# Attention values split inside their own head pair: a change to the emission order of a hybrid decoder block

## The chip, the cores and the metric

The kernel runs on one core of one Trainium2 chip. The metric is the device time of one execution in microseconds (us). Six queues matter in what follows. TensorE (PE) multiplies matrices; its weight loads are shown apart as PEld. VectorE (DVE), ScalarE (ACT) and GpSimd (POOL) do elementwise work. SyncE (SP) issues nearly all DMA transfers. Each engine takes its instructions strictly in the order in which the program emits them, so an instruction that waits holds up everything behind it on its engine.

## The reference

The block mixes tokens by dilated sliding-window attention and by a causal convolution, joins the two with sigmoid gates, and then runs a SwiGLU feed-forward network. Only the attention matters here. There are three groups of eight heads of width 64, with a window and a dilation for each group. Every group gives an output and a log denominator, and the three groups are merged per head with a softmax over these denominators:

```python
s = jnp.einsum('brnqhd,brnkhd->brnhqk', qb, kb) * (Dh ** -0.5) + bias
s = jnp.where(valid[:, None], s, NEG_INF)
lse = jax.nn.logsumexp(s, axis=-1)
p = jnp.exp(s - lse[..., None])
o = jnp.einsum('brnhqk,brnkhd->brnqhd', p, vb)
...
alpha = jax.nn.softmax(jnp.stack(lses, axis=0), axis=0)
o = jnp.einsum('gbsh,gbshd->bshd', alpha, jnp.stack(outs, axis=0))
```

Sequence length and model width are 1024; all inputs are float32.

## The kernel before

Every product is made of three matrix products of a rounded high part and a low part (`hi*hi + hi*lo + lo*hi`), so each operand has to be split by two instructions first: a copy that rounds (`hi`, on ACT) and a subtraction (`lo`, on DVE or POOL).

The stages follow each other: projections and the convolution, then the value projections (`v`, L843 to L877), two late gates, the convolution's output product (eight column tiles, `unit`, matmuls at L287, L289, L291), the attention's output product, the mixing product and the feed-forward part. Attention has no stage of its own. It is a Python generator, `attention` (L882), and `beat` advances it by one `yield` after about every third matmul of the value projections (`RATE` 0.33) and after about every 1.5 matmuls later (0.66). Its instructions are thus threaded between the filler matmuls on every engine, in the order of emission. There is no scheduler beyond that. A second clock, `tick`, comes once for each three matmuls and drives the background generators: weight splits, `conv_norm`, `conv_split` and the merges.

Attention works through 12 head pairs, called (group, pair) here: (0,0) to (2,3), eight query blocks `u` each, 96 steps `s` in all. One step emits the scores of block `s` (`att_s`: four matmuls at L937, bias and minimum on DVE at L940), the exponentials of block `s-1` (`att_e`, ACT L950), the transposes of block `s-3` (`att_t`: PE L973, split on ACT L978 and DVE L979) and the product with the values of block `s-4` (`att_p`: PE L994 and L996, reduction on DVE L1001). After `att_e` of the last block of a pair in groups 0 and 1 the statistics go to memory (`tokens_out`, L959 or L963), and after `att_p` of the last block the outputs do.

Three helpers feed a pair:

- `stacks` (from L790) loads queries and keys of the next pair: four query loads of 256 KB (L799, L800), two key loads of 512 KB (L801) and the bias (L458). POOL then copies the query halves across partitions in eight casts (L806, L807). It is emitted when the running pair has passed its block 1 (`u == 2`).
- `values` (L820) loads the values of the next pair (L826, L829 or L831) from the memory tensor to which `v` stored them (L850).
- `value_parts` (L834) splits one half of these values: a copy on ACT (L839) and a subtraction on POOL (L840).

In the kernel before, `values` for the next pair is emitted at block 4 of the running pair, and its two `value_parts` at blocks 6 and 7 of the running pair. For the very first pair the load is emitted only when `conv_norm` has ended, and the generator then lets 12 beats pass.

In group 2, when a pair is done, `others` (L811) loads statistics (L815) and outputs (L817) of the two other groups, and `merge` (L1010) is started as a background generator: minimum over the groups (L1018), weights (L1019 to L1025), three scaled outputs (L1029; group 0 on POOL, the others on DVE), two additions (L1031, L1033), and eight transposes with their split (L1040, L1043, L1044).

SP issues DMAs in emission order. The transfers share eight semaphore lanes in turn, so a transfer also waits for the one issued eight places before it.

Of the kernel before, what the change touches and what calls it, by code (L numbers as in the profile page):

```python
# [54 lines left out]
def f(ap):  # L55
    return ap.bitcast(F32)


class Build:
# [730 lines left out]
    def stacks(self, g, hp):  # L790
# [17 lines left out]
        st = self.tiny(96, "stat", 3).rearrange("p (g u e) -> p g u e", g=3, u=8)  # L808
        return [g, hp, ops, bt, st, []]

    def others(self, p):  # L811

        hp, st, outs = p[1], p[4], p[5]
        for i in range(2):
            self.nc.sync.dma_start(st[:, i], self.d_st[i, hp].rearrange("(p u) e -> p u e", u=8))  # L815
            outs.append(self.slot())
            self.nc.sync.dma_start(outs[i].rearrange("p (u e) -> p u e", u=8),  # L817
                                   self.d_att[i, hp].rearrange("(p u) e -> p u e", u=8))
# [63 lines left out]
    def attention(self, after):  # L882

        live, s, total = {}, 0, 96
        order = [(g, hp) for g in range(3) for hp in range(4)]
        nxt, cur, u, x, V = self.stacks(*order.pop(0)), None, 8, None, []
        while s < total + self.LP:
            if s < total:
                if x is None and nxt and u > 3 and nxt[0] * 2 + nxt[1] // 2 < self.vn:
                    x = self.values(*nxt[:2])  # L890
                elif u in (6, 7) and x is not None:
                    V.append(self.value_parts(x, u - 6))
                if u == 8:
                    while after in self.gens or nxt[0] * 2 + nxt[1] // 2 >= self.vn:
                        yield 0
                    if x is None:
                        x = self.values(*nxt[:2])
                        for _ in range(12):
                            yield 0
                    while len(V) < 2:  # L900
                        V.append(self.value_parts(x, len(V)))
                    now, cur, u, nxt, x, V = V, nxt, 0, None, None, []
                live[s] = a = {}
                self.att_s(a, cur, now, u)
                u += 1
                if u == 8:
                    cur[2] = cur[3] = now = None
                if u == 2 and order:
                    nxt = self.stacks(*order.pop(0))
            if s % 8 == 1 and s > 64 and live[s - 2]["p"][0] == 2:  # L910
                self.others(live[s - 2]["p"])
            if 0 <= s - 1 < total:
                self.att_e(live[s - 1])
            yield 0
            if 0 <= s - self.LT < total:
                self.att_t(live[s - self.LT])
                yield 0
            if 0 <= s - self.LP < total:
                yield from self.att_p(live.pop(s - self.LP))
            s += 1  # L920
# [89 lines left out]
    def merge(self, hp, st, O):  # L1010


        nc = self.nc
        t = self.tiny(96, "mrg", 2)
        m, r = (t[:, i * 16:(i + 1) * 16].rearrange("p (u e) -> p u e", u=8) for i in range(2))
        w = t[:, 48:].rearrange("p (g u e) -> p g u e", g=3, u=8)
        low, tot = st[:, :, :, 0:2], st[:, :, :, 2:4]
        nc.vector.tensor_reduce(m, low.rearrange("p g u e -> p u e g"), AX.X, OP.min)  # L1018
        nc.vector.tensor_tensor(w, low, m.unsqueeze(1).to_broadcast([128, 3, 8, 2]), op=OP.subtract)  # L1019
        nc.scalar.activation(t[:, 48:], t[:, 48:], AF.Exp, scale=-1.0)  # L1020
        yield 2
        nc.vector.tensor_tensor(tot, tot, w, op=OP.mult)
        nc.vector.tensor_reduce(m, tot.rearrange("p g u e -> p u e g"), AX.X, OP.add)
        nc.vector.reciprocal(r, m)
        nc.vector.tensor_tensor(w, w, r.unsqueeze(1).to_broadcast([128, 3, 8, 2]), op=OP.mult)  # L1025
        for g in range(3):
            y = O[g].rearrange("p (u h c) -> p u h c", u=8, h=2)
            a = w[:, g].unsqueeze(3).to_broadcast([128, 8, 2, 64])
            (nc.gpsimd if g == 0 else nc.vector).tensor_tensor(y, y, a, op=OP.mult)  # L1029
            yield 1  # L1030
        nc.vector.tensor_tensor(O[1], O[1], O[2], op=OP.add)  # L1031
        yield 1
        nc.vector.tensor_tensor(O[0], O[0], O[1], op=OP.add)  # L1033
        yield 3
        hi, lo = self.slot(F32R), self.slot(F32R)
        for h in range(2):
            ps = self.bank("t")
            for i in range(4):
                u = h * 4 + i
                nc.tensor.transpose(ps[:, i * 128:(i + 1) * 128], O[0][:, u * 128:(u + 1) * 128], self.ident)  # L1040
            y = ps.rearrange("p (u m) -> p u m", u=4)
            a, b = (x.rearrange("p (m u) -> p u m", u=8)[:, h * 4:h * 4 + 4] for x in (hi, lo))
            nc.scalar.copy(a, y)  # L1043
            nc.vector.tensor_tensor(b, y, f(a), op=OP.subtract)  # L1044
            yield 2
        self.OT[hp] = hi, lo

# [154 lines left out]
def build(ctx, tc, aps):  # L1202
    B = Build(ctx, tc, aps)
# [93 lines left out]
    B.finish(conv)  # L1297
    assert bl not in B.gens
    B.banks(g=2, s=2, t=2, o=2)
    B.OT, B.merges = {}, []  # L1300
    cn = B.bg(B.conv_norm())
    att = B.attention(cn)
# [11 lines left out]
    for n in range(LATE):  # L1314
        w = B.weights(late[n])
        s = B.slot()
# [10 lines left out]
    def gate_load(d):  # L1327
        c = B.slot()
        nc.sync.dma_start(c, d)
        return c  # L1330

    nxt = gate_load(B.d_gc[0])
    ws = {}

    for n, hf in [(0, 0), (1, 0), (0, 1), (1, 1)] + [(n, hf) for n in range(2, 8) for hf in range(2)]:
        if hf == 0:
            ws[n] = B.weights(co[n])
            mg[n] = nxt
            nxt = gate_load(B.d_gc[n + 1]) if n < 7 else (gate_load(B.d_ga[0]), gate_load(B.d_gc[0]))
# [4 lines left out]
        ps = B.unit(ws[n], B.rhs(B.cop[hf]), KT)  # L1344
# [21 lines left out]
    for n in range(8):  # L1366
# [4 lines left out]
        for hf in range(2):  # L1371
            s = slice(hf * H, (hf + 1) * H)
            ps = B.unit(w, lambda kt: tuple(x[:, s] for x in B.OT[kt]), 4)
            nc.vector.tensor_tensor(c[:, s], ps, c[:, s], op=OP.mult)
            nc.vector.tensor_tensor(c[:, s], c[:, s], y[:, s], op=OP.add)
            x = B.slot(F32R)
# [4 lines left out]
    y = None  # L1381
# [173 lines left out]
    for j in range(PLAIN, FT):  # L1555
        s = [None, None]
        p, odd = divmod(j, 2)
# [231 lines left out]
```

## Time and profile before

| what | value |
|---|---|
| time, median of 3 runs | 1787.02 us (1786.26 to 1789.1) |
| the profiled execution | 1787.76 us, span 1786.0 us |
| PE busy, share of the span | 1725.8 us, 97% |
| DVE, ACT, POOL busy | 70%, 44%, 28% |
| first and last value matmul (L863) starts | 563.9 us and 803.6 us |
| first score matmul (L937), last value product (L994) start | 635.1 us and 950.4 us |
| transposes of the merges (L1040) | 902.1 us to 968.0 us |

The span starts at the first instruction. A row of the timeline gives start, duration, engine, line of the kernel, operation, and in brackets how long the engine had sat idle before and what released it. A row of the windows gives the busy time of each engine in a stretch, the granted TensorE clock as a share of full speed (PEclk), the busy share of the DMA engines, and the rate. Matmuls overlap, so a row's duration is longer than the distance to the next one.

### The profile page before, as it was taken

The numbers are of one execution on the slowest core, as the hardware profiler recorded it, in microseconds if no ns is written. First come the engines' busy times: TensorE is split into PE (matmuls) and PEld (weight loads), VectorE is DVE, ScalarE is ACT, GpSimd is POOL, SyncE is SP. The second block draws the span as 40 slices with busy tenths as digits, with TensorE's granted clock in tenths as the row PEclk, the third lists the DMA queues.
The fourth block names the chain that finished last, engine by engine and source line by source line (L and its number), as shares of the span: only waits on it lengthen the run. The fifth ranks groups of instructions, "written<-read, shape, count | busy, mean of one in ns | idle before, by whom it ended". The sixth has DMA issues, their size and how long they took to land.

```text
span 1786.0 us, 24511 instructions
## 1 busy us (share of the span) xinstructions
PE 1725.8 (97%) x8698; PEld 1462.3 (82%) x8698; DVE 1251.7 (70%) x2198; ACT 790.9 (44%) x1549; POOL 505.8 (28%) x357
## 2 busy tenths in 40 slices
PE   8989999999999989999898999999999999999998
PEld 6768888887777989998687888888888888878886
DVE  6899867899996546555676475586566565567686
ACT  6344344334433456556553145653333333353453
POOL 0067777877773223332320040040000000000000
PEclk9999999999999989999889999999999999999999
DMA  4333334556667576667753753203223223395234
GB/s 159 140 118 123 119 118 147 154 165 174 186 165 224 161 215 181 190 186 232 264 182 104 261 193 107 100 36 123 89 89 140 90 89 124 130 333 170 95 134 148
DMA packets 185783, 274.94 MB, mean 154 GB/s; under 512 B 56113, under 2 KB 107948, under 8 KB 185660
## 3 DMA queue, kind: packets, MB, share of 16 engines
q1 hardware_dynamic: 185020, 272.74, 47.6%
q8 instruction: 68, 1.11, 0.3%
q10 hardware_dynamic: 576, 0.56, 0.1%
q14 instruction: 55, 0.45, 0.1%
q0 software_dynamic: 64, 0.07, 0.0%
HBM read 183.76 MB, written 94.28 MB: 156 GB/s over the span
## 4 chain that ended last, share of the span: by engine, by line
PE 64%; DVE 5%; DMA 3%; ACT 2%; issue 1%; POOL 0%; SPq 0%; DVEq 0%; ACTq 0%; POOLq 0%
PE p L1673 12%; PE p L305 8%; PE p L303 8%; PE p L304 8%; PE p L1409 5%; PE p L291 3%; PE p L289 3%; PE p L287 3%; PE p L865 3%; PE p L867 3%; PE p L863 2%; PE p L937 2%; PE p L973 1%; PE p L996 1%; DMA b<-dv 1%
## 5 line engine op out<-in xcount | busy, mean ns | idle before, releaser
L303 PE MATMUL p<-b,b 128*128 128x512 f32 x1204 | 471.1, 391 | 14.0 <-DVE c L777 7.3
L305 PE MATMUL p<-b,b 128*128 128x512 f32 x1204 | 470.1, 390 | 0.4 <-POOL b L180 0.4
L304 PE MATMUL p<-b,b 128*128 128x512 f32 x1204 | 470.0, 390 | 0.0
L303 PEld LDWEIGHTS p<-b,b 128*128 128x128 f32 x1204 | 226.9, 188 | 64.8 <-DVE c L777 9.2
L305 PEld LDWEIGHTS p<-b,b 128*128 128x128 f32 x1204 | 227.0, 189 | 48.9 <-POOL b L180 1.5
L304 PEld LDWEIGHTS p<-b,b 128*128 128x128 f32 x1204 | 226.9, 188 | 46.7
L179 ACT CAST b<-b 128x1024 fp32r<-128x1024 f32 x129 | 135.6, 1051 | 181.0 <-POOL b L200 71.0
L1673 PE MATMUL p<-b,b 128*128 128x512 f32 x924 | 209.7, 389 | 1.5 <-DVE c L1582 1.5
L180 POOL TENSOR_TENSOR b<-b,b 128x1024 fp32r<-128x1024 f32 x72 | 175.6, 2438 | 115.7 <-ACT b L179 99.7
L1673 PEld LDWEIGHTS p<-b,b 128*128 128x128 f32 x924 | 173.3, 188 | 37.9 <-DVE c L1582 1.9
L637 DVE SCALAR_TENSOR_TENSOR p<-b,par,p 128x511 f32<-128x511 f32 (+14 forms) x232 | 163.6, 738 | 0.0
L180 DVE TENSOR_TENSOR b<-b,b 128x1024 fp32r<-128x1024 f32 x57 | 69.7, 1223 | 123.8 <-ACT b L179 123.8
L287 PE MATMUL p<-b,b 128*128 128x512 f32 x368 | 152.7, 415 | 0.8 <-DVE b L1348 0.8
L291 PE MATMUL p<-b,b 128*128 128x512 f32 x368 | 150.9, 410 | 0.0
L289 PE MATMUL p<-b,b 128*128 128x512 f32 x368 | 150.5, 409 | 0.0
L1052 DVE TENSOR_TENSOR b<-c,b 128x512 fp32r<-128x512 f32 x125 | 90.7, 736 | 39.7 <-ACT b L1051 39.4
L863 PE MATMUL p<-b,b 128*128 128x256 f32 x384 | 114.7, 299 | 2.2 <-DVE c L783 2.2
L865 PE MATMUL p<-b,b 128*128 128x256 f32 x384 | 114.7, 299 | 0.9 <-DVE b L173 0.9
L867 PE MATMUL p<-b,b 128*128 128x256 f32 x384 | 114.0, 297 | 0.0
L1051 ACT CAST b<-c 128x512 fp32r<-128x512 f32 x125 | 76.5, 618 | 56.0 <-DVE c L355 17.6
L979 DVE TENSOR_TENSOR c<-p,c 128x256 fp32r<-128x256 f32 (+1 forms) x96 | 52.3, 545 | 68.5 <-ACT c L978 60.2
L1409 PE MATMUL p<-b,b 128*128 128x512 f32 x384 | 88.9, 391 | 0.0
(222 smaller groups left out, 3042.6 us busy)
## 6 DMA issues: line engine op xcount, KB each, us to landing
b<-w_in SPq DMA_DIRECT2D x53, 512.0 KB, 4.8
b<-w_fi SPq DMA_DIRECT2D x44, 512.0 KB, 4.8
dk<-c SPq DMA_DIRECT2D x96, 128.0 KB, 2.5
dq<-c SPq DMA_DIRECT2D x96, 128.0 KB, 2.4
b<-dq SPq DMA_DIRECT2D x48, 256.0 KB, 7.1
b<-dk SPq DMA_DIRECT2D x24, 512.0 KB, 8.5
dqS<-c SPq DMA_DIRECT2D x44, 256.0 KB, 2.2
b<-w_fo SPq DMA_DIRECT2D x44, 256.0 KB, 5.4
```

The lines of the kernel that those rows point to most:

```text
L180: self.wsplit.tensor_tensor(lo, x, f(hi), op=OP.subtract)
L287: nc.tensor.matmul(ps, hi[:, s], a, start=kt == 0, stop=False)
L289: nc.tensor.matmul(ps, hi[:, s], b, start=False, stop=False)
L291: nc.tensor.matmul(ps, lo[:, s], a, start=False, stop=kt == nk - 1)
L303: nc.tensor.matmul(ps, hi[:, s], a, start=first and kt == 0, stop=False, skip_group_check=True)
L304: nc.tensor.matmul(ps, hi[:, s], b, start=False, stop=False, skip_group_check=True)
L305: nc.tensor.matmul(ps, lo[:, s], a, start=False, stop=kt == 3, skip_group_check=True)
L637: nc.vector.scalar_tensor_tensor(A[i][:, j:], src[i][:, :H - j], w[i], A[i][:, j:], op0=OP.mult, op1=OP.add)
L865: nc.tensor.matmul(o, a, lo[:, s], start=False, stop=False)
L867: nc.tensor.matmul(o, b, hi[:, s], start=False, stop=kt == KT - 1)
L1409: nc.tensor.matmul(banks[tt][nh], st, wt[:, nh * H:(nh + 1) * H], start=bool(kt == 0 and a), stop=bool(kt == KT - 1 and b))
L1673: nc.tensor.matmul(acc[t], x, y, start=first and e == 0, stop=last and e == 2, skip_group_check=True)
```

## The change

It has five parts.

1. `value_parts` moves from blocks 6 and 7 of the pair before to blocks 2 and 3 of the pair itself (after their scores, when `u` has become 3 and 4). In emission order these follow `stacks` of the next pair. The load stays at block 4 of the pair before, but the condition on `u` is gone, so that the first pair's values are loaded as soon as they are stored.
2. The 12 beats that the first pair let pass are gone.
3. The loads of the two other groups' statistics become `other_stats`, emitted at block 5 of the group-2 pair; the loads of their outputs come one step later than before.
4. `merge` waits two ticks more at its start and two more ahead of its transposes. Several references are dropped earlier, which gives buffers back.
5. One bank with the tag `s` is taken and left unused when the banks of this stage are laid out, so that the later users of that tag get the two banks in the other order.

```diff
+    def other_stats(self, p):
+        for i in range(2):
+            self.nc.sync.dma_start(p[4][:, i], self.d_st[i, p[1]].rearrange("(p u) e -> p u e", u=8))
+
     def others(self, p):
-        hp, st, outs = p[1], p[4], p[5]
+        hp, outs = p[1], p[5]
         for i in range(2):
-            self.nc.sync.dma_start(st[:, i], self.d_st[i, hp].rearrange("(p u) e -> p u e", u=8))
             outs.append(self.slot())
...
+        def there():
+            return nxt[0] * 2 + nxt[1] // 2 < self.vn
+
         while s < total + self.LP:
             if s < total:
-                if x is None and nxt and u > 3 and nxt[0] * 2 + nxt[1] // 2 < self.vn:
+                if x is None and nxt and there():
                     x = self.values(*nxt[:2])
-                elif u in (6, 7) and x is not None:
-                    V.append(self.value_parts(x, u - 6))
                 if u == 8:
-                    while after in self.gens or nxt[0] * 2 + nxt[1] // 2 >= self.vn:
+                    while after in self.gens or x is None:
+                        if x is None and there():
+                            x = self.values(*nxt[:2])
                         yield 0
-                    if x is None:
-                        x = self.values(*nxt[:2])
-                        for _ in range(12):
-                            yield 0
-                    while len(V) < 2:
-                        V.append(self.value_parts(x, len(V)))
-                    now, cur, u, nxt, x, V = V, nxt, 0, None, None, []
+                    V, cur, u, nxt = [], nxt, 0, None
                 live[s] = a = {}
-                self.att_s(a, cur, now, u)
+                self.att_s(a, cur, V, u)
                 u += 1
+
+                if u in (3, 4):
+                    V.append(self.value_parts(x, u - 3))
+                    if u == 4:
+                        x = None
+                if u == 6 and cur[0] == 2:
+                    self.other_stats(cur)
                 if u == 8:
-                    cur[2] = cur[3] = now = None
+                    cur[2] = cur[3] = cur = V = None
                 if u == 2 and order:
                     nxt = self.stacks(*order.pop(0))
-            if s % 8 == 1 and s > 64 and live[s - 2]["p"][0] == 2:
-                self.others(live[s - 2]["p"])
+            if s % 8 == 2 and s > 64 and live[s - 3]["p"][0] == 2:
+                self.others(live[s - 3]["p"])
...
     def merge(self, hp, st, O):
         nc = self.nc
+        yield 2
...
         nc.vector.tensor_tensor(O[1], O[1], O[2], op=OP.add)
+        O[2] = y = a = None
         yield 1
         nc.vector.tensor_tensor(O[0], O[0], O[1], op=OP.add)
-        yield 3
+        O[1] = None
+        yield 5
...
             nc.vector.tensor_tensor(b, y, f(a), op=OP.subtract)
+            ps = y = a = b = None
             yield 2
...
     B.banks(g=2, s=2, t=2, o=2)
+
+    B.bank("s")
```

More of the change, by code (lines that the diff above doesn't have):

```diff
@@ L885, in attention @@
         order = [(g, hp) for g in range(3) for hp in range(4)]
-        nxt, cur, u, x, V = self.stacks(*order.pop(0)), None, 8, None, []
+        nxt, cur, u, x, V = self.stacks(*order.pop(0)), None, 8, None, None
+        def there():
+            return nxt[0] * 2 + nxt[1] // 2 < self.vn
         while s < total + self.LP:
             if s < total:
-                if x is None and nxt and u > 3 and nxt[0] * 2 + nxt[1] // 2 < self.vn:
+                if x is None and nxt and there():
                     x = self.values(*nxt[:2])
-                elif u in (6, 7) and x is not None:
-                    V.append(self.value_parts(x, u - 6))
                 if u == 8:
-                    while after in self.gens or nxt[0] * 2 + nxt[1] // 2 >= self.vn:
+                    while after in self.gens or x is None:
+                        if x is None and there():
+                            x = self.values(*nxt[:2])
                         yield 0
-                    if x is None:
-                        x = self.values(*nxt[:2])
-                        for _ in range(12):
-                            yield 0
-                    while len(V) < 2:
-                        V.append(self.value_parts(x, len(V)))
-                    now, cur, u, nxt, x, V = V, nxt, 0, None, None, []
+                    V, cur, u, nxt = [], nxt, 0, None
                 live[s] = a = {}
-                self.att_s(a, cur, now, u)
+                self.att_s(a, cur, V, u)
                 u += 1
+                if u in (3, 4):
[4 more added lines that the diff above has]
+                    self.other_stats(cur)
                 if u == 8:
-                    cur[2] = cur[3] = now = None
+                    cur[2] = cur[3] = cur = V = None
                 if u == 2 and order:
                     nxt = self.stacks(*order.pop(0))
-            if s % 8 == 1 and s > 64 and live[s - 2]["p"][0] == 2:
-                self.others(live[s - 2]["p"])
+            if s % 8 == 2 and s > 64 and live[s - 3]["p"][0] == 2:
+                self.others(live[s - 3]["p"])
             if 0 <= s - 1 < total:
```

## The prediction

> **What bounds the kernel now.** I read the page's busy times first, then the windows of the stretch in which attention runs, then the list of waits, then the timeline at the longest waits.
>
> ```profile
> span 1786.0 us, 24511 instructions
> PE 1725.8 (97%) x8698; PEld 1462.3 (82%) x8698; DVE 1251.7 (70%) x2198; ACT 790.9 (44%) x1549; POOL 505.8 (28%) x357
> ```
>
> TensorE is the bound: only 60 us of the span are left without a matmul. The change adds or removes no instruction of PE, DVE, ACT or POOL and no DMA; it alters their order. So the time can move only by PE's idle time and by its clock.
>
> ```profile
> 640.00:660.00 20.00, 13.42 (x91) 13.22 (x92) 7.03 (x21) 13.06 (x37) 8.99 (x11) 0.74 0.61 148
> 700.00:720.00 20.00, 20.00 (x175) 20.00 (x175) 13.27 (x40) 12.61 (x39) 5.34 (x7) 1.00 0.49 118
> 880.00:900.00 20.00, 17.51 (x85) 14.80 (x85) 14.44 (x48) 8.46 (x34) 9.06 (x6) 0.79 0.39 121
> 900.00:920.00 20.00, 18.16 (x102) 15.23 (x101) 14.50 (x46) 10.95 (x37) 7.46 (x8) 0.89 0.74 223
> ```
>
> After the span's share come PE, PEld, DVE, ACT and POOL, then the granted clock. PE has holes at the start of attention and in group 2, and none in group 0 (700 to 720). Where there are holes the clock falls too.
>
> ```profile
> 784.00:786.00 2.00, 1.27 (x10) 0.92 (x9) 1.08 (x3) 2.00 (x7) 0.88 (x2) 1.00 0.32 90
> ...
> 830.00:835.00 5.00, 4.25 (x28) 3.48 (x28) 2.82 (x7) 4.94 (x15) 2.49 (x2) 1.00 0.48 168
> 855.00:860.00 5.00, 2.97 (x11) 2.40 (x11) 2.68 (x9) 4.68 (x16) 2.54 (x2) 0.76 1.03 417
> 860.00:865.00 5.00, 5.00 (x21) 4.26 (x21) 3.81 (x12) 3.07 (x12) 0.00 (x0) 0.56 0.60 224
> 875.00:880.00 5.00, 1.51 (x7) 0.91 (x6) 1.00 (x4) 1.20 (x4) 2.48 (x5) 0.80 1.04 406
> 880.00:885.00 5.00, 5.00 (x18) 4.31 (x19) 1.63 (x7) 0.85 (x5) 0.00 (x0) 0.51 0.24 97
> 960.00:965.00 5.00, 2.13 (x10) 1.43 (x8) 4.91 (x5) 0.00 (x0) 0.00 (x0) 1.00 0.63 215
> ```
>
> Idle 0.7 us (784, 830) leaves the clock at 1.00. Idle 2.0 us (855) costs (0.24 + 0.44) x 5 = 3.4 us of clock, idle 3.5 us (875) again (0.20 + 0.49) x 5 = 3.4 us. The 2.9 us at 960 cost none, so the fall is usual and not certain. I charge 3 us for a wait of 2 us or more, in five cases of six.
>
> ```profile
> POOL b L806 <- DMA b<-dq: 112.2, 18, 31.8
> ACT b L839 <- DMA b<-dv: 23.4, 8, 8.1
> PE p L973 <- ACT c L950: 8.0, 1, 8.0
> ```
>
> Total, count and longest. ACT waits 23.4 us for value loads; POOL waits 112.2 us for query loads, ahead of its casts. The second wait is harmless today, and it is what my forecast turns on.
>
> **The change part by part.** *What it removes.* ACT copies values soon after their load was issued, and PE stands behind ACT:
>
> ```profile
> 847.66 1.07 SPq L831 DMA_DIRECT2D b<-dv  x1
> 855.32 0.62 ACT L839 CAST b<-b 128x512 fp32r<-128x512 f32 x1 [3.10 <-DMA b<-dv]
> 878.30 0.22 DVE L1018 TENSOR_REDUCE mrg<-stat 128x16 f32<-128x48 f32 x1 [4.55 <-DMA stat<-dst]
> ```
>
> The load takes 7.7 us, the copy follows two blocks after it. In the new order six or seven blocks lie between, some 20 us (a pair's eight blocks take 25.3 us from the value product at 677.07 to the one at 702.37, both quoted below), so this wait goes: 0.75 us at 830, 0.73 at 784, and 2.0 + 3.4 us at 855, together 6.9. The statistics' wait (878) goes as well, since their load now comes five blocks before the merge: 3.5 + 3.4 = 6.9. From the spaced merge I take half of the 2.9 us at 960: 1.4. Between 885 and 920 another 8 us of idle and clock are lost in waits that I can't give to one edit; I let half go: 4. Removed: 6.9 + 6.9 + 1.4 + 4 = 19.2 us.
>
> *What it adds in every pair.* In the program order of the changed kernel, POOL does the eight casts of pair k+1 first and then the value subtractions of pair k, where before the subtractions of pair k stood far ahead of their use. The first value product of pair k on PE waits for the first of them. Queued behind a waiting cast on POOL, then, is what PE needs next; behind PE's wait are all filler matmuls. Pair (0,2) shows the race:
>
> ```profile
> 687.83 0.36 SPq L959 DMA_DIRECT2D dst<-stat  x1
> 688.28 0.54 SPq L799 DMA_DIRECT2D b<-dq  x1
> ...
> 694.38 0.60 POOL L806 CAST b<-b 64x512 fp32r<-64x512 f32 x1 [7.83 <-DMA b<-dq]
> ...
> 702.13 0.61 POOL L807 CAST b<-b 64x512 fp32r<-64x512 f32 x1
> ...
> 702.37 0.22 PE L994 MATMUL p<-b,c 128*128 128x128 f32 x1
> ...
> 707.59 1.27 POOL L840 TENSOR_TENSOR b<-b,b 128x512 fp32r<-128x512 f32 x1 [4.85 <-ACT b L839]
> ```
>
> The statistics of the last pair go out at 687.83, the stacks of the next follow, and the last cast ends at 702.74. A subtraction of 1.3 us behind it ends at 704.1; PE wants it at 702.37 and waits 1.7 us. Nothing in the change hastens the stacks: both kernels put them behind the same write of statistics, which ACT's exponentials release. So the wait of a pair is the start of its last cast, plus 0.61, 0.05 and 1.29, less the start of its first value product.
>
> ```profile
> 676.71 0.61 POOL L807 CAST b<-b 64x512 fp32r<-64x512 f32 x1
> 677.07 0.22 PE L994 MATMUL p<-b,c 128*128 128x128 f32 x1
> ...
> 800.51 0.22 PE L994 MATMUL p<-b,c 128*128 128x128 f32 x1
> 802.93 0.61 POOL L807 CAST b<-b 64x512 fp32r<-64x512 f32 x1
> ...
> 847.44 0.22 PE L994 MATMUL p<-b,c 128*128 128x128 f32 x1
> 853.98 0.61 POOL L807 CAST b<-b 64x512 fp32r<-64x512 f32 x1
> ...
> 873.20 0.22 PE L994 MATMUL p<-b,c 128*128 128x128 f32 x1
> 877.07 0.61 POOL L807 CAST b<-b 64x512 fp32r<-64x512 f32 x1
> ```
>
> From such rows, first (0,1) and last (2,1) shown, the nine pairs between them give 1.6, 1.7, 2.9, 1.5 | 3.7, 4.4, 5.4 | 8.5, 5.8 = 35.5 us; (2,2) gives 0.2, and (2,3) has no stacks behind it. Six of these are over 2 us: clock, 5 x 3 = 15 us. The lower end for a pair is about nothing: the fourth query load leaves 2.8 us after the statistics' write, lands at the median of 7.1 us, then five casts (3.3) and the subtraction (1.35) end 14.6 us after the write, and PE comes 14.5 us after it (702.37 less 687.83). The upper end is 8.5 each. I take each pair's own row.
>
> ```profile
> b<-dq SPq DMA_DIRECT2D x48, 256.0 KB, 7.1
> ```
>
> *The start.* The 12 beats fewer bring attention 36 value matmuls forward. Their starts lie 0.12 us apart, so 4.3 us: scores at 630.8 instead of 635.13.
>
> ```profile
> 634.89 0.28 PE L867 MATMUL p<-b,b 128*128 128x256 f32 x1
> 635.01 0.28 PE L863 MATMUL p<-b,b 128*128 128x256 f32 x1
> ...
> 643.58 1.14 ACT L839 CAST b<-b 128x512 fp32r<-128x512 f32 x2 [8.10 <-DMA b<-dv]
> ...
> 646.58 0.48 PE L973 MATMUL p<-ident,c 128*128 128x128 f32 x1 [7.97 <-ACT c L950]
> ...
> 650.82 0.61 POOL L807 CAST b<-b 64x512 fp32r<-64x512 f32 x1 [0.33 <-DMA b<-dq]
> ```
>
> Before, PE idles 8.0 us here, as ACT waits for the first values. After, those values are long there, and PE comes to its first value product after 21 value matmuls (2.5 us), five score groups and two transposes (some 3 us) and what ACT needs, near 637.5. It then waits for the casts of pair (0,1). Their last query half landed at 650.8; with one 512 KB load fewer ahead of it, at 226 GB/s 2.3 us sooner. One cast, four more and a subtraction (4.6 us) make 653.1: idle 15.6 us for 8.0, so 7.6 worse.
>
> *The rest at nothing.* The two additional merge pauses and dropped references issue nothing; what hides them are the column tiles beside the merges. SP has the statistics' loads earlier, eight issues of under a microsecond that stand ahead of convolution loads; later outputs may make the merge wait instead, bounded by the 3.5 us at 875 either way. The turned bank adds no instruction; its first user was not waited for by PE, so 0, with 0.75 us (the hole at 830) as either end.
>
> *Sum.* 7.6 + 35.5 + 15 - 19.2 = 38.9 us on the profiled execution's 1787.76 us: 1826.7. That execution is 0.7 us over the median of 1787.02, so 1826.
>
> The Trainium skill, "TensorE: Matmul & The Clock Gate", section "HAM oscillation — how this bites in real kernels", gives as its rule no idle gap over about 3.4 us, and the section on the clock gate a warm-up of about 3.4 us at half speed. By that only the five waits over 3.4 us would cost clock, 1.7 us each, an estimate of 8.5 us in place of 15 and a time of 1820. The trace disagrees at 855: 2.0 us of idle were enough, and 3.4 us were lost.
>
> **The rivals.** (a) *Faster.* The stacks land as early as their lower end, the subtraction is ready at PE's arrival, and all of it hinges on the casts' end lying 1.35 us or more before the first value product. For it speaks that four pairs miss by only 1.5 to 1.7 us or 2.9; against it that all nine miss, and groups 1 and 2 by 3.7 to 8.5. The start stays. 7.6 - 19.2 = -11.6: 1776. (b) *Slower by little.* Group 0 and (1,0) get through, the other five miss by half (14 us), two clock falls (6): 7.6 + 14 + 6 - 19.2 = 8.4: 1796. (c) *Much slower.* In group 2 the copy on ACT takes a buffer that the merge's addition gives back, and the merge now loads its outputs later; ACT waits for DVE, DVE for the DMA. At the 3.5 us of the row at 875 with its clock, 7 us for each of three merges: 1847. (d) *It does nothing.* The wait moves from ACT to POOL at equal price: 1787. For that the pairs' waits would have to add up to no more than 12 us.
>
> **How the numbers follow.** My forecast has 0.54, (a) 0.12, (b) 0.20, (c) 0.09, (d) 0.05. About 0.2% (3.6 us) is what a measurement of this kernel can tell from no change. Slower: 0.54 + 0.20 + 0.09 = 0.83; within it 0.05; faster 0.12. The forecast's own range runs from 1805 (no clock falls, 15 less, and the group 0 waits gone, 6) to 1847. To leave out no more than 0.2, the range takes in (b), (d) and half of (c): 1786 to 1848.
>
> **What would show it.** Right: waits on PE at its value product released by POOL's subtraction, ten of them, the longest near 635 to 653; POOL's subtraction released by the cast before it and not by ACT; no wait of ACT's value copy for its load; no wait of the merge's minimum for statistics; a granted clock below 1.00 in stretches of group 1 that had 1.00. Wrong: PE full in 660 to 780 as now, the last cast of a pair ending over 1.4 us before the first value product, or a start with less than 8 us of idle.

## The result and the profile after

The changed kernel takes 1837.3 us (median of 4 runs, 1836.52 to 1842.77) against 1787.92 us for the kernel before, run beside it: a ratio of 1.0275 (95% interval 1.0256 to 1.0294), so it is 2.7% slower. The profiled execution took 1837.51 us.

The first fence has the page's span and its row for TensorE after the change (busy us, share of the span, instructions).

```profile
span 1835.7 us, 24474 instructions
PE 1733.2 (94%) x8698; PEld 1469.4 (80%) x8698; DVE 1255.0 (68%) x2198; ACT 792.0 (43%) x1549; POOL 503.0 (27%) x357
```

The matmuls are the same 8698. The span grew by 1835.7 - 1786.0 = 49.7 us. PE's idle time went from 60.2 to 102.5 us, so 42.3 of these are idle. The other 7.4 are PE busy time, 1733.2 for 1725.8: the same matmuls at a slower clock.

Where it lies is seen in the windows of 20 us that were shown of before (length, PE, PEld, DVE, ACT, POOL, granted clock, DMA share, GB/s):

```profile
640.00:660.00 20.00, 9.30 (x63) 9.30 (x63) 3.69 (x12) 3.28 (x10) 7.38 (x10) 0.62 0.41 108
700.00:720.00 20.00, 17.92 (x155) 17.71 (x155) 11.31 (x37) 10.09 (x33) 6.53 (x8) 1.00 0.43 117
880.00:900.00 20.00, 15.14 (x80) 13.31 (x80) 6.94 (x28) 7.61 (x26) 5.54 (x7) 0.73 0.31 106
900.00:920.00 20.00, 8.16 (x52) 6.84 (x50) 8.38 (x30) 10.07 (x34) 3.71 (x7) 0.78 1.01 279
```

The stretch 700 to 720, full before, has a hole of 2 us at full clock. The start (9.3 of 20 us busy) and group 2 (8.2 of 20 us after 900) have the large ones. The list of waits names one releaser (total, times, longest):

```profile
POOL b L806 <- DMA b<-dq: 208.1, 18, 40.2
...
PE p L1002 <- POOL b L843: 59.3, 10, 15.1
...
ACT b L842 <- DVE b L1040: 6.2, 1, 6.2
```

PE now waits ten times, 59.3 us in all, at its first value product (L1002, before L994) for POOL's subtraction (L843, before L840). POOL waits 208.1 us for query loads, where it waited 112.2. No wait of ACT's value copy for its load and none of the merge for statistics is left; a new one of 6.2 us on the merge's addition is there, at 944 us. The timeline gives the ten waits one by one (length in the brackets), and for the last of them what stood ahead of it on SP and POOL:

```profile
650.70 0.47 PE L1002 MATMUL p<-b,c 128*128 128x128 f32 x1 [15.08 <-POOL b L843]
...
679.63 0.33 PE L1002 MATMUL p<-b,c 128*128 128x128 f32 x1 [1.28 <-POOL b L843]
...
707.30 0.33 PE L1002 MATMUL p<-b,c 128*128 128x128 f32 x1 [2.08 <-POOL b L843]
...
734.35 0.33 PE L1002 MATMUL p<-b,c 128*128 128x128 f32 x1 [1.45 <-POOL b L843]
...
761.89 0.33 PE L1002 MATMUL p<-b,c 128*128 128x128 f32 x1 [2.03 <-POOL b L843]
...
787.37 0.33 PE L1002 MATMUL p<-b,c 128*128 128x128 f32 x1 [2.02 <-POOL b L843]
...
815.77 0.47 PE L1002 MATMUL p<-b,c 128*128 128x128 f32 x1 [3.39 <-POOL b L843]
...
848.76 0.48 PE L1002 MATMUL p<-b,c 128*128 128x128 f32 x1 [6.20 <-POOL b L843]
...
884.86 0.47 PE L1002 MATMUL p<-b,c 128*128 128x128 f32 x1 [11.32 <-POOL b L843]
...
899.65 1.20 SPq L1131 DMA_DIRECT2D c<-dact  x2
900.90 0.46 SPq L1343 DMA_DIRECT2D b<-dgc  x1
901.41 0.42 SPq L161 DMA_DIRECT2D b<-w_co  x1
...
902.35 0.66 SPq L799 DMA_DIRECT2D b<-dq  x1
...
911.45 0.61 POOL L806 CAST b<-b 64x512 fp32r<-64x512 f32 x1 [25.42 <-DMA b<-dq]
...
920.61 0.61 POOL L807 CAST b<-b 64x512 fp32r<-64x512 f32 x1
921.30 2.49 POOL L843 TENSOR_TENSOR b<-b,b 128x512 fp32r<-128x512 f32 x2
922.62 0.48 PE L1002 MATMUL p<-b,c 128*128 128x128 f32 x1 [14.45 <-POOL b L843]
```

The first row is the start of attention, then follow the pairs (0,1) to (2,1). The rows from 899.65 to 922.62 show the whole chain: the query loads of the next pair leave SP behind loads of the convolution and of a weight; POOL stands 25.4 us at the first cast, does the casts as the loads land, then the subtraction, and PE goes on 1.3 us after that began. Two shorter waits of group 2, 1.79 us at 951 and 1.74 us at 963, are not released by POOL.

### The profile page after: what moved, and what is told of

Its sections match the earlier page's. It is cut to its first block, busy times and chain, and to the rows that moved or that the text cites. A ratio compares the mean times of both kernels' runs of the same rounds, so it can differ in the third digit from the quotient of the medians.

```text
span 1835.7 us, 24474 instructions
## 1 busy us (share of the span) xinstructions
PE 1733.2 (94%) x8698; PEld 1469.4 (80%) x8698; DVE 1255.0 (68%) x2198; ACT 792.0 (43%) x1549; POOL 503.0 (27%) x357
## 4 chain that ended last, share of the span: by engine, by line
PE 60%; DMA 5%; DVE 4%; POOL 3%; issue 2%; ACT 2%; SPq 1%; DVEq 0%; POOLq 0%; ACTq 0%
PE p L1687 11%; PE p L303 8%; PE p L305 8%; PE p L304 8%; PE p L1423 4%; PE p L291 3%; PE p L287 3%; DMA b<-dq 3%; PE p L289 3%; PE p L868 2%; PE p L866 2%; PE p L870 2%; PE p L945 2%; PE p L981 1%; PE p L1002 1%
## 5 line engine op out<-in xcount | busy, mean ns | idle before, releaser
L303 PE MATMUL p<-b,b 128*128 128x512 f32 x1204 | 471.8, 392 | 13.4 <-DVE c L777 6.8
L305 PE MATMUL p<-b,b 128*128 128x512 f32 x1204 | 471.0, 391 | 0.4 <-POOL b L180 0.4
L304 PE MATMUL p<-b,b 128*128 128x512 f32 x1204 | 470.9, 391 | 0.0
L1687 PE MATMUL p<-b,b 128*128 128x512 f32 x924 | 209.8, 389 | 1.5 <-DVE c L1596 1.5
L287 PE MATMUL p<-b,b 128*128 128x512 f32 x368 | 152.3, 414 | 0.0
L289 PE MATMUL p<-b,b 128*128 128x512 f32 x368 | 150.9, 410 | 0.0
L291 PE MATMUL p<-b,b 128*128 128x512 f32 x368 | 150.3, 408 | 0.0
L1002 PE MATMUL p<-b,c 128*128 128x128 f32 x280 | 66.0, 261 | 62.0 <-POOL b L843 59.3
L1002 PEld LDWEIGHTS p<-b,c 128*128 128x128 f32 x280 | 56.3, 201 | 67.4 <-POOL b L843 62.0
```

The costliest lines, as they stand in the source:

```text
L287: nc.tensor.matmul(ps, hi[:, s], a, start=kt == 0, stop=False)
L289: nc.tensor.matmul(ps, hi[:, s], b, start=False, stop=False)
L291: nc.tensor.matmul(ps, lo[:, s], a, start=False, stop=kt == nk - 1)
L303: nc.tensor.matmul(ps, hi[:, s], a, start=first and kt == 0, stop=False, skip_group_check=True)
L304: nc.tensor.matmul(ps, hi[:, s], b, start=False, stop=False, skip_group_check=True)
L305: nc.tensor.matmul(ps, lo[:, s], a, start=False, stop=kt == 3, skip_group_check=True)
```

## The experiments

The theory after the result: the casts of the next pair stand in POOL's queue ahead of the subtractions of the running pair, and PE waits for POOL, which waits for the query loads. The rivals: the later value splits cost time by themselves; the removed beats, the statistics or the merges carry the loss. All times are medians. The first eight experiments ran on one chip, beside the kernel before at 1786.23 us, the last four on another, beside it at 1785.73 us; between the two groups only ratios to the kernel before are compared.

**The casts behind the subtractions.**

```diff
-        for s in (slice(0, H), slice(H, T)):     # in stacks
-            for k, a, b in ops:
-                nc.gpsimd.tensor_copy(a[low, s], f(a[top, s]))
-                nc.gpsimd.tensor_copy(b[top, s], f(b[low, s]))
+    def casts(self, p):                          # the same casts
...
                     V.append(self.value_parts(x, u - 3))
                     if u == 4:
                         x = None
+                        if nxt:
+                            self.casts(nxt)
```

The loads stay where they are.

> The changed kernel, but the eight casts of the next pair are emitted right after the second value subtraction of the running pair instead of with their loads; the loads stay where they are. Theory (POOL's subtraction stands behind casts that wait for query loads): the ten waits of 59.3 us on PE go, and the clock that they cost with them, some 12 to 15 us; 1837 - 59 - 14 gives about 1765, below the kernel before. Rival (the loss comes from attention standing 36 matmuls earlier, or from SP's order): the waits on PE get another releaser and the time stays over 1805.

Measured: 1762.63 us (1761.31 to 1766.75), a ratio to the kernel before of 0.9871 (0.9855 to 0.9888). That is 23.6 us less than the kernel before and, by the two ratios (1.0275 - 0.9871, of 1786), 72 us less than the changed kernel. It beats both, and no other kernel here came out lower. Its timeline at a pair of group 0 on POOL:

```profile
678.01 1.29 POOL L846 TENSOR_TENSOR b<-b,b 128x512 fp32r<-128x512 f32 x1 [15.69 <-ACT b L845]
...
682.06 0.61 POOL L811 CAST b<-b 64x512 fp32r<-64x512 f32 x1
...
687.10 0.61 POOL L812 CAST b<-b 64x512 fp32r<-64x512 f32 x1
```

POOL now waits for the copy on ACT, early; the eight casts follow without a gap, since their loads landed meanwhile. Of PE's waits from 600 to 1100 us the longest group is another one:

```profile
PE p L951 <- DMA b<-dk: 2.9, 2, 2.6
```

All ten waits of 59.3 us are gone. By the spans of the two profiles (1835.7 and 1764.7) the difference of 71.0 us is 56.3 us of idle and 14.7 us of PE busy time, 1733.2 for 1718.5. So the order on POOL carries the loss, and more than the whole of it. The rival that the late splits cost time by themselves falls.

**The values alone, on the kernel before.**

```diff
-                elif u in (6, 7) and x is not None:
-                    V.append(self.value_parts(x, u - 6))
...
+                if u in (3, 4):
+                    V.append(self.value_parts(x, u - 3))
```

The load at block 4, the beats, statistics, merges and banks are those of before.

> The kernel before with one part of the change alone: both value splits move to blocks 2 and 3 of their own pair. The 12 beats, the statistics, the merges and the banks stay as before. Theory: the ten waits behind the casts appear as in the changed kernel, 50 to 60 us, with 10 us of clock, while only the values' DMA waits (7 us) go; 1787 + 55 + 10 - 7 gives about 1840 (1825 to 1850). Rival (this part is harmless alone, and the earlier start or the statistics bring the loss): 1780 to 1795.

Measured: 1826.07 us, a ratio of 1.0228 (1.0212 to 1.0245). The first part alone gives 2.28 of the 2.75% that the whole change loses. It lies at the low end of what was expected, and its list of PE's waits shows why (total, times, longest):

```profile
PE p L994 <- POOL b L840: 40.6, 10, 10.2
```

Ten waits again, but the start's is 8.8 us behind another of 4.3, and those of the first two pairs of group 2 are 5.0 and 10.2 us. The other four parts together make it slower by another 0.5%, though some of them gain on the kernel before (below). It is these two waits of group 2 that grow most with them, from 15.2 us together to 25.8.

**The stacks one block earlier.** The casts stay ahead of the subtractions.

```diff
-                if u == 2 and order:
+                if u == 1 and order:
                     nxt = self.stacks(*order.pop(0))
```

> The changed kernel, but loads and casts of the next pair are emitted one block earlier, after block 0 instead of block 1, and so ahead of the write of the last pair's statistics. Theory (the wait of a pair is the end of the casts against the first value product): each pair's wait falls by a block's time, 2.5 to 3.3 us, or more since the small-packet write no longer stands ahead: the six waits of 1.3 to 3.4 us go, 6.2, 11.3 and 14.5 us fall to about 3, 8 and 11, the start stays near 15: 37 us of waits for 59, with 6 us of clock 1837 - 22 - 6 = about 1809. Rival (the waits are set by something that moves along, such as the queue's bandwidth): waits as before, 1835.

Measured: 1789.72 us, a ratio of 1.0027 (1.0015 to 1.0040), some 19 us better than expected. The waits of PE for POOL that are left:

```profile
647.68 0.47 PE L1002 MATMUL p<-b,c 128*128 128x128 f32 x1 [15.07 <-POOL b L843]
...
850.98 0.33 PE L1002 MATMUL p<-b,c 128*128 128x128 f32 x1 [3.63 <-POOL b L843]
...
861.55 0.49 SPq L799 DMA_DIRECT2D b<-dq  x1
...
870.07 0.33 SPq L161 DMA_DIRECT2D b<-w_co  x1
...
876.55 0.47 PE L1002 MATMUL p<-b,c 128*128 128x128 f32 x1 [3.42 <-POOL b L843]
```

Seven of the ten are gone, and the two of group 2 fell from 11.3 and 14.5 to 3.6 and 3.4 us. A block is some 3.2 us long (25.3 us for a pair's eight), yet two waits shrank by 8 and 11. SP's rows give a likely reason: the query loads of the second leave at 861.55, ahead of the weight's load at 870.07, where in the changed kernel they left behind it; from there to the product it is 15.0 us and was 20.3. The start is unmoved: in both kernels SP comes to these query loads only behind the stores of the values (L853), and the first of them leaves 0.09 us after the last store was issued (at 630.99 us in the changed kernel, 628.44 here).

**The statistics and the merges alone, on the kernel before.** The edits are parts 3 and 4 of the change as they stand.

> The kernel before with the statistics loaded ahead, the outputs one step later and the merges spaced out as in the change, and nothing else of it. Theory (the prediction's removed terms): the wait of the merge's minimum for statistics goes (3.5 us of idle and 3.4 us of clock), half of the idle at the last merge (1.4 us) and some of what follows: 1775 to 1781. Rival (the wait only moves on to the outputs' loads): 1787, within 3 us.

Measured: 1780.61 us, a ratio of 0.9971 (0.9959 to 0.9983), 5.6 us less. It is as expected, and less than the forecast counted for these parts (6.9 + 1.4, and 4 of the unnamed losses). ACT and PE show what is late next:

```profile
880.86 0.62 ACT L842 CAST b<-b 128x512 fp32r<-128x512 f32 x1 [3.77 <-DMA b<-dv]
...
882.56 0.47 PE L999 MATMUL p<-b,c 128*128 128x128 f32 x1 [6.20 <-ACT c L983]
```

The wait for the statistics is gone, and at the same place ACT waits for the next pair's values, with PE behind it for 6.2 us.

**The start alone.** From here on the first experiment's kernel is the base. Only the second pair's casts are put ahead of the first pair's subtractions again:

```diff
                     nxt = self.stacks(*order.pop(0))
+                    if s < 8:
+                        self.casts(nxt)
...
-                        if nxt:
+                        if nxt and not (s < 8):
                             self.casts(nxt)
```

> The changed kernel with all casts behind the second value subtraction, except those of the second pair, which stand ahead of the first pair's subtractions as in the change: only the wait at the start is put back. Theory (the wait costs its own length and a slow clock behind it): the changed kernel waited 15.1 us there, and its stretch of 20 us from 640 us ran at a clock of 0.62, so 1762.6 + 15 + 5 = about 1782 us (1776 to 1787). Rival (the idle at the start is taken back later, since the value projections are late anyway): within 4 us of 1762.6.

Measured: 1780.95 us (1778.7 to 1784.86), 18.3 us more than the base. One wait is back:

```profile
649.77 0.48 PE L1010 MATMUL p<-b,c 128*128 128x128 f32 x1 [15.61 <-POOL b L846]
```

Theory right, rival wrong: the idle at the start isn't taken back. By the profiles it cost 13.0 us of idle and 1.5 us of clock (PE busy 1720.0 for 1718.5). The base's profiled execution was the slowest of its four, though, and the medians leave 5.3 us beside the idle, so whether the 5 us of clock that were expected were too many stays open.

**Group 2 alone.** The same edit with `s >= 64` in the place of `s < 8`.

> The changed kernel with all casts behind the second value subtraction, except in group 2, where they stand ahead of the subtractions as in the change. Theory (the waits of group 2 are long because its stacks stand behind the convolution's loads in SP's queue): two waits of 11.3 and 14.5 us come back, and the clock that falls behind them, 1785 to 1795 us. Rival (those two waits were long because the waits of groups 0 and 1 had moved the pairs against the column tiles): only the 5 to 9 us each of the forecast, 1774 to 1781 us.

Measured: 1789.64 us (1786.71 to 1791.9), 27.0 us more than the base (20.2 by the spans of the profiles).

```profile
838.08 0.48 PE L1010 MATMUL p<-b,c 128*128 128x128 f32 x1 [10.53 <-POOL b L846]
...
853.70 0.42 SPq L161 DMA_DIRECT2D b<-w_co  x1
...
854.64 0.66 SPq L799 DMA_DIRECT2D b<-dq  x1
...
865.05 0.60 POOL L811 CAST b<-b 64x512 fp32r<-64x512 f32 x1 [25.79 <-DMA b<-dq]
...
875.04 0.48 PE L1010 MATMUL p<-b,c 128*128 128x128 f32 x1 [14.60 <-POOL b L846]
```

The two waits come back at nearly the size they have in the changed kernel (10.5 and 14.6 for 11.3 and 14.5), with no wait in groups 0 and 1 ahead of them. So the earlier waits did not make them long; in SP's queue the query loads stand behind the convolution's and the weight's in both kernels. That this order is the whole reason was not tried: no kernel moved those loads alone.

**The values with the casts behind them, on the kernel before.** The edits of the first two experiments together, without parts 2 to 5.

> The kernel before with only the value splits moved to their own pair, and the casts of the next pair behind the second of these subtractions; the 12 beats, the statistics' loads, the merges and the banks stay as before. Theory (moving the values costs nothing itself, and the rest of the change brings the 5.6 us of the statistics and merges): 1762.6 + 5.6 = 1768 us (1765 to 1773). Rival (the 12 beats or the banks carry part of the gain of 1762.6): 1775 to 1782 us. If the values' move has a loss of its own: 1784 or more.

Measured: 1777.48 us (1776.52 to 1778.4), a ratio of 0.9951 (0.9937 to 0.9965). The time lies in the rival's range: 1768 was expected of plain addition, and some 9 us are missing. The trace names neither the beats nor the banks for most of it, but the statistics, which this kernel loads as before:

```profile
873.28 0.22 DVE L1024 TENSOR_REDUCE mrg<-stat 128x16 f32<-128x48 f32 x1 [8.45 <-DMA stat<-dst]
...
874.34 0.47 PE L1000 MATMUL p<-b,c 128*128 128x128 f32 x1 [7.32 <-ACT c L984]
```

Here the wait for values is gone, and the wait for the statistics stands alone: 8.45 us on DVE, 7.3 on PE. With parts 3 and 4 and without the earlier values (above) it was the other way round. Neither part gains its full price without the other.

**Both: casts behind and stacks earlier.** The edits of the first and the third experiment.

> The changed kernel with the casts behind the second value subtraction and the loads of queries and keys one block earlier as well. Theory (with the casts behind, no wait on the loads is left but 2.9 us of the scores on a key load): 1758 to 1763 us. Rival (earlier loads collide with the loads of the values or of the weights): 1766 to 1775 us.

Measured: 1770.19 us, 7.6 us more than with the casts behind alone. The rival is right that earlier loads cost something; PE waits 2.5 and 2.1 us for ACT at 806 and 863 us, where the base has no such wait. At the first place ACT stands idle 5.6 us ahead of the copy of a weight (L172, 803.61); the profile names no releaser for it, so the transfer behind it stays open. The two waits are 4.6 us, and the base's own 2.6 us for a key load is nearly gone (0.6), so most of the 7.6 us is not accounted for.

**The bank.** The first experiment's kernel without `B.bank("s")`.

> The changed kernel with the casts behind the second value subtraction, and without the fifth part: the bank of the tag s isn't taken ahead. Theory (the forecast's: the banks cost nothing in this stage): 1762.6 us, within 2 us. Rival (the banks hold the later stages apart and carry part of what the kernel with the own pair and the casts behind alone lacked): 1766 to 1772 us.

Measured: 1769.1 us (1764.32 to 1774.25), a ratio of 0.9913 (0.9891 to 0.9935), against 0.9871 (0.9855 to 0.9888) with the bank on the other chip. The spans of the profiles differ little (1765.4 and 1764.7 us), but the base's profiled execution was its slowest. The theory, that the bank costs nothing, does not hold in the trace. With the bank as before, the first matmul of the value projections waits for VectorE, in the kernel before (first row) as here (second row):

```profile
563.93 0.53 PE L863 MATMUL p<-b,b 128*128 128x256 f32 x1 [2.24 <-DVE c L783]
...
564.71 0.39 PE L869 MATMUL p<-b,b 128*128 128x256 f32 x1 [2.24 <-DVE c L783]
```

All eight kernels with the bank as before have this wait of 2.24 us, and none of the six with the bank turned; in the first experiment PE goes on to this matmul without a gap (562.97 us). From 560 to 640 us PE is busy for 78.66 us there and for 76.75 here, so the bank is worth 1.9 us of PE's time in this stage. What it is worth in the whole stays open, since scatter and chip differ: by the medians it is some 6 us.

**All but the beats, the early load and the bank.** The kernel before with parts 1, 3 and 4 and the casts behind; the load at block 4 and the 12 beats as before.

> The kernel before with the values in their own pair, the casts behind them, the statistics ahead and the merges spaced; the load of a pair's values stays at its place of before with the 12 beats of the first pair, and the bank isn't taken ahead. If the missing 9.3 us (1777.5 less 5.6 of the statistics and merges, less 1762.6) lie in the start: 1772 us, within 2.5 us, with about 5 us of idle behind 640 us. If the parts hinder or help each other otherwise: below 1767 or above 1776 us.

Measured: 1766.58 us (1764.93 to 1768.59), a ratio of 0.9896 (0.9878 to 0.9915). It lies just below the 1767 that were set for parts that help each other, with runs on both sides of it. Parts 3 and 4 gained 0.29% on the kernel before, and on the one with values and casts in order they gain from 0.9951 to 0.9896, 0.55%. That they gain more there is what the medians say; the intervals are too wide to show it. At the start PE waits 4.4 us here; without the beats (first experiment) there is none, but the ratios 0.9896 and 0.9871 overlap in their intervals, so what the beats and the bank are worth together with the casts in order is not told apart from nothing by the times; by the medians it is some 4 us.

**The statistics alone, and the merges alone,** each on the kernel before.

> The kernel before with the statistics' loads at block 5 alone. Theory (the forecast's term: the wait of 6.9 us of VectorE for the statistics held TensorE up by as much): 1779 to 1782 us. Rival (the merge waits for the outputs' loads next, and the wait only moves): 1784 to 1788 us.

> The kernel before with the merges' two waits of two ticks and the earlier dropped references alone. Theory (the statistics carry the 5.6 us that both together gained): 1785 to 1788 us. Rival (the spacing carries them, since it gives the statistics time to land): 1779 to 1783 us.

Measured: 1784.64 us, a ratio of 0.9994 (0.9981 to 1.0008), for the statistics, and 1782.04 us, a ratio of 0.9978 (0.9966 to 0.9991), for the merges. The statistics alone gain nothing that can be told. Their trace shows the new wait:

```profile
875.68 0.32 SPq L834 DMA_DIRECT2D b<-dv  x1
...
887.28 0.62 ACT L842 CAST b<-b 128x512 fp32r<-128x512 f32 x1 [9.62 <-DMA b<-dv]
...
888.98 0.47 PE L999 MATMUL p<-b,c 128*128 128x128 f32 x1 [10.68 <-ACT c L983]
```

The value load leaves SP at 875.7, the copy on ACT waits 9.6 us for it, and PE 10.7 us. The rival was right that the wait only moves, but not in where it moves to: what PE waits for are the values and not the outputs. By the medians the spacing carries the larger part of the 5.6 us, though the two intervals overlap. Its trace doesn't show from where: the wait at the merges' transposes, which was 3.1 us, is 0.7, but PE has a new wait of 3.5 us at 913 for a merge's split on VectorE, and one of 6.8 us at 885 where it had 3.5.

## Why the prediction was right, point by point

The forecast was right in sign and mechanism, and 11 us too low.

- **PE's wait at the value product for POOL, ten times.** Right: ten waits, released by L843, which ran right behind a cast. That the casts' place is the cause is shown by the first experiment.
- **The start, 15.6 us idle for 8.0.** Right: 15.1 measured; put back alone it cost 18.3 us by the medians, 14.5 by the profiles. Both ends of the wait came some 2 us sooner than forecast (PE at 635.6 for 637.5, the subtraction's end at 650.7 for 653.1), so that the size came out is in part luck.
- **The nine pairs, 35.5 us.** Right in kind, 44.2 measured. Groups 0 and 1 came to 18.4 for 21.2. Group 2 was mis-sized: 11.3 and 14.5 us in place of 8.5 and 5.8. The step that failed is "I take each pair's own row". It took the last cast's place in the trace of before. There the weight's load stood ahead of the query loads of (2,2) too, but left SP 10.3 us sooner than they did:

```profile
853.38 0.40 SPq L161 DMA_DIRECT2D b<-w_co  x1
...
863.67 0.49 SPq L799 DMA_DIRECT2D b<-dq  x1
```

In the changed kernel the two are 0.9 us apart (901.41 and 902.35). From the first of these query loads to the last cast it was 13.4 us and is now 18.3, and the first leaves 5.8 us ahead of PE's arrival at its value product (908.2), where it left 9.5 us ahead (873.20). These 4.9 and 3.7 us are what the row was short of. That the nearness of the other loads delays the landing fits them, but no kernel shows it alone. The forecast counted the statistics' loads ahead of convolution loads, and left out that the stacks and those loads are emitted by different generators, whose place against each other shifts. With the first part alone the two waits of group 2 came to 15.2 us, near the 14.3 of their rows, but as 5.0 and 10.2 us; so the sum was near by luck, and the rest came with the other parts.

- **The clock, five falls of 3 us.** Right in the balance, which alone was measured: of 15 added and 6.8 removed (twice 3.4), 8.2 us more PE busy time was forecast, and 7.4 measured. Against the first experiment's kernel, which has none of the ten waits, it is 14.7.
- **Removed, 19.2 us.** The two named waits went. Of the idle part, 8.4 us in the named places (0.75, 0.73, 2.0, 3.5, 1.4) and up to 4 more, 9.0 us are found: start and pairs add 7.1 + 44.2 us, and PE's idle time grew by only 42.3. So the term "I let half go: 4" was too much. Short waits such as the 1.79 and 1.74 us at 951 and 963 stand in the place of others. Some 1.5 us of the 9.0 belong to the bank (next point). As a single edit the statistics brought 1 us and not 6.9, since the value load is late next; together with the earlier values, they and the spaced merges bring 0.55%, some 10 us.
- **The rest at nothing.** The spaced merges were not nothing: 3.7 us on the kernel before, where 1.4 was charged for them among the removed terms. For the bank, "its first user was not waited for by PE" fails: with the bank as before PE waits 2.24 us at 563.93, and with it turned it does not.
- **The rivals.** (a) and (b) hinged on the casts' end lying 1.35 us or more ahead of the value product; in no pair from (0,1) to (2,1) did it. Nearest came (0,1), with 0.13 us (678.22 against 678.35). Of (c), ACT's copy did wait for the merge's addition, 6.2 us at 944, but PE's wait at its next product (946) was 0.9 us, not 7.

The sum of the misses on the spans, against the 38.9 us forecast: pairs +8.7, start -0.5, removed idle +3.4 (12.4 forecast, with the 4 taken as idle, and 9.0 found), clock -0.8, together 10.8, and 49.7 - 38.9 = 10.8.

Shares of what lies between the changed kernel and the one with the casts behind (72 us by the ratios): the start 19 and group 2 27, each put back alone. The other 26 are left for the seven waits of groups 0 and 1, which add up to 18.4 us, their clock, and what the parts do to each other; those seven were not put back alone, so this share is only a remainder. The spans of the profiles give 14.5 and 20.2 of 71.0, but they are single executions, and that of the kernel with the casts behind was its slowest.

## What to carry to other kernels

When an instruction is moved past others on an in-order queue, look at what those others wait for: a wait that was harmless becomes the wait of whoever needs the moved instruction. The cure here was to keep the loads early and to emit only the waiting casts behind the work that PE needs next, which made a loss of 2.7% a gain of 1.3%. Two waits that end near each other in one stage are not priced singly, since either is hidden by the other.

## What the runs showed of the hardware

I had charged 3 us of clock for five of six waits of 2 us or more. The waits of about 2 us in the changed kernel stand on both sides (windows of 5 us around two of them and behind them; the clock is the third column from the end):

```profile
705.00:710.00 5.00, 2.92 (x25) 2.71 (x25) 1.88 (x6) 1.52 (x5) 3.35 (x4) 1.00 0.73 195
710.00:715.00 5.00, 5.00 (x46) 5.00 (x45) 2.97 (x10) 3.73 (x11) 0.00 (x0) 1.00 0.02 3
...
785.00:790.00 5.00, 2.98 (x19) 2.77 (x19) 1.19 (x3) 1.95 (x6) 3.41 (x4) 0.84 1.06 338
790.00:795.00 5.00, 5.00 (x39) 5.00 (x38) 2.06 (x10) 1.68 (x6) 0.00 (x0) 0.82 0.02 4
...
817.00:822.00 5.00, 5.00 (x25) 5.00 (x25) 1.62 (x6) 2.72 (x10) 0.00 (x0) 0.50 0.00 1
822.00:827.00 5.00, 5.00 (x43) 5.00 (x43) 2.72 (x9) 1.89 (x6) 0.00 (x0) 0.95 0.00 0
```

The wait of 2.08 us at 707 left the clock at 1.00; the wait of 2.02 us at 787 brought it to 0.84 and 0.82, (0.16 + 0.18) x 5 = 1.7 us. The wait of 3.39 us at 815 was followed by 5 us at 0.50. So length alone does not decide it. The wait of 2.24 us at the first value matmul shows this at one place: over the 4 us from 564 us on, the clock was 0.57 to 0.67 in five of the eight kernels that have the wait, and 1.00 in three. What else decides it is not shown. The Trainium skill, "TensorE: Matmul & The Clock Gate", section "HAM oscillation — how this bites in real kernels", states a rule of no idle gaps over about 3.4 us; this trace shows falls behind shorter ones.
